# Three instead of four seven-product K-pairs in the query, key and pooled groups, and side splits in two steps

## The chip, the cores and the metric

The kernel runs on one core of a Trainium2 chip. The metric is the device time of one execution in microseconds; lower is better. The engines are named as in the profile: PE (TensorE matrix products, PEld its weight loads), DVE (VectorE), ACT (ScalarE), POOL (GpSimd) and SP (the queue that issues the DMAs). Each engine works through its own instructions strictly in the order in which the program gives them.

## The reference

One decoder layer on 256 tokens of width 2048, all in float32:

```
h   = rms_norm(x)
proj = h @ w_in                      # 2048 x 13312: q,k,v of attention A, u, q,k,v of C, 3 gates
ya  = softmax attention (8 heads of 128)
yb  = sliding-window means minus identity, one 256x256 map per group
yc  = stick-breaking attention (8 heads of 128)
m   = sum_b sigmoid(gate_b) * (y_b @ w_br_b)
x   = x + m @ w_out
h   = rms_norm(x)
x   = x + (silu(h @ w_gate) * (h @ w_up)) @ w_down       # 2048 x 5632
out = rms_norm(x)
```

## The kernel before

Each float32 operand is split into a high part that PE can take (fp32r) and the low rest, and a product is made of three PE instructions: high by high, low by high, high by low. Such an instruction has 128 rows, 128 columns of weights (here the activations) and 512 columns that stream (here the weight matrix).

The work is a list of groups; a group is one block of output columns over all of K. Most use the plain form (class `Group`). The groups of two 512-column blocks at once (class `Squares`: query A, key A and u of the first projection, the gates of branches b and c, and gate and up of the SwiGLU) run over eight pairs of K-tiles. A pair of kind `N` makes eight 128x512 products, thus 24 PE instructions, from one loaded raw tile: one high split on ACT (L446, 128x2048), one low split on DVE (L452, 128x2048). A pair of kind `W` makes seven products, thus 21 instructions, in two units: `Wp` (9) and `Ws` (12). It needs three sums of the raw weights on DVE (L442, L443, L444), two high splits (1536 and 2048 wide) and two low splits (1536 and 2048 wide), and of the activations four difference blocks where `N` needs two (`differences`, L150 to L170). The kinds of the eight pairs stand in two strings:

```
FFN_KINDS = "NNWNWNWN"
GATE_KINDS = "NWNWNWWN"
```

The first, with three `W`, holds for the SwiGLU groups, the second, with four, for every `Squares` group of w_in.

A `Squares` group collects its sums in seven of the eight PSUM banks; the eighth is left for side work. The first two blocks are freed early, by `squares_early` (ACT L474, DVE L475, L476).

What surrounds the groups is the list `side`: generators entered with `beside(gen, after, lag)`. After each unit on PE, `step_side` takes the first generator that is due and runs it to its next `yield`; its instructions land at that place in each engine's order. Side work is the activations' differences (`add_differences`, one K-pair a step), the attention heads, the pooling, the turning of `m` and of the hidden state (`turn` in `br`, L898, and in `output`, L954), and the end of each SwiGLU block (`finish`, L1001). The last three transpose on PE into a free bank and then split out of that bank: ACT writes the high part (L108), DVE subtracts it (L109), and the bank is free once both have read it. Between units the loop also issues the splits of units up to four ahead (`high` on ACT, `low` on DVE).

The order of the stages is: value A, then query A, key A and u (`Squares`), the projections of branch C (plain, with attention A and pooling beside them), gates and branch products, `output`, then eleven SwiGLU blocks in four parts, each with its share of the down projection.

Of the kernel before, what the change touches and what calls it, by code (L numbers as in the profile page):

```python
# [51 lines left out]
def trunk(ctx: ExitStack, tc: tile.TileContext, x, norm_mix, norm_ffn, w_in, w_pool, pool_scale,  # L52
# [43 lines left out]
    def f32(ap):  # L96
        return ap.bitcast(F32)
# [7 lines left out]
    def split(hi, lo, src, scale=None):  # L105
# [4 lines left out]
        else:  # L110
            nc.scalar.activation(hi, src, AF.Copy, scale=scale)
            nc.vector.scalar_tensor_tensor(lo, src, scale, f32(hi), OP.mult, OP.subtract)

    def branch():
        return slot([HEADS, SEQ], F32R), slot([HEADS, SEQ], F32R)

# [10 lines left out]
    class Halves:  # L127
# [22 lines left out]
        def differences(self, p, a):  # L150

            e = wk().rearrange("p (n s) -> p n s", s=P)
            n = 4 if self.kinds[p] == "W" else 2
            if n == 2:
                nc.vector.tensor_tensor(e[:, 0:2], a[:, :, 0], a[:, :, 1], OP.subtract)
            else:
                f = a.rearrange("p k t s -> p (k t) s")
                nc.vector.tensor_tensor(e[:, 0:2], f[:, 1:2].to_broadcast([P, 2, P]), f[:, 0:4:3], OP.subtract)
                nc.vector.tensor_tensor(e[:, 2], f[:, 0], e[:, 1], OP.subtract)
                nc.vector.tensor_tensor(e[:, 3], f[:, 2], e[:, 2], OP.subtract)  # L160
            for i, (tile, used) in enumerate(self.tiles):
                if used + 2 * n <= 16:
                    break
            else:
                i = len(self.tiles)
                tile, used = (late_slot if late and i < 1 else slot)([16, P], F32R), 0
                self.tiles.append(None)
            self.tiles[i] = tile, used + 2 * n
            self.ext[p] = tile, used, n
            split(tile[:, used:used + n], tile[:, used + n:used + 2 * n], e[:, 0:n])  # L170

        def add_differences(self, p):
            a = wk()
            hi, lo = self.pair(p)
            nc.vector.tensor_tensor(a.rearrange("p (k s) -> p k s", k=2), f32(hi), f32(lo), OP.add)
            self.differences(p, a.rearrange("p (k t s) -> p k t s", k=2, t=NT))

        def fill(self, p, pt, scales):

            a = wk()  # L180
            for j in range(2):
                k = slice(j * SEQ, (j + 1) * SEQ)
                nc.scalar.activation(a[:, k], pt[:, k], AF.Copy, scale=scales[j])
            split(*self.pair(p), a.rearrange("p (k s) -> p k s", k=2))
            self.differences(p, a.rearrange("p (k t s) -> p k t s", k=2, t=NT))


    xt = [slot([D_MODEL]) for _ in range(NT)]
# [65 lines left out]
    rstd1 = [st1[:, t, 9:10] for t in range(NT)]  # L254
    rstd2 = [st2[:, t, 9:10] for t in range(NT)]

    xT = Halves(GATE_KINDS)

    def prepare_x(kt):
        transposed(xT(kt), [xt[t][:, kt * P:(kt + 1) * P] for t in range(NT)], ncols[:, kt:kt + 1])  # L260
# [6 lines left out]
        side.append([clock[0] + after, lag, gen])  # L267

    def step_side():
        for e in side:  # L270
            if e[0] <= clock[0]:
                side.remove(e)
                try:
                    e[0] = clock[0] + (next(e[2]) or e[1])
                    side.append(e)
                except StopIteration:
                    pass
                return True
        return False

    def finish_side():
        while side:
# [298 lines left out]
    def proj_in(col, after, before=None, turned=False):  # L581
        return Group(lambda: xT, range(KT), w_in, 0, col, after, before, turned=turned)

    def in_pair(c0, finish, then=None):

        early = []

        def load(raw, p):
            nc.sync.dma_start(raw.rearrange("p j n c -> p j (n c)"),
                              w_in[2 * p * P:2 * (p + 1) * P, c0:c0 + 2 * CH].rearrange("(j p) c -> p j c", p=P))  # L590

        def begin(b):
            early.append(squares_early(b))

        def end(b):
            yield from finish(squares_end(b, early[0]))

        def before():
            cap[0] = 9

        def after(b):
            beside(end(b), after=2, lag=1)
            if then:
                then()

        return Squares(lambda: xT, load, after, begin, before, GATE_KINDS)


    live = {}
# [229 lines left out]
            yield  # L839

    def start_block():
        xT.tiles, xT.ext = [], {}
        make_bias()
        live["ya"] = branch()
        for hp in range(HEADS // 2):
            beside(block_attention(hp), after=8 + 4 * hp, lag=3)
        beside(pooling(), after=16, lag=2)
# [17 lines left out]
    def gate_pair(i, b):  # L865

        def finish(c):
            for t in range(NT):
                for n in range(2):
                    nc.scalar.activation(c[t][n], c[t][n], AF.Sigmoid, scale=rstd1[t])  # L870
            for n in range(2):
                gates[2 * i + n] = [c[t][n] for t in range(NT)]
            yield

        return in_pair(7 * WIDTH + b * D_MODEL + 2 * i * CH, finish)

    def br(n, b, plain=False):
        key = ("ya", "yb", "yc")[b]

        def lhs():  # L880
            y = live[key]
            return lambda kt: (y[0][:, kt, :], y[1][:, kt, :])

        def before():
            if n == 0 and b == 0:
                finish_side()
                open_late()
                beside((xT.add_differences(p) for p in range(KT // 2)), after=4, lag=2)
            if n % 2 == 0 and b == 0:
                both = slot([2, NT, CH])  # L890
                m.extend([both[:, i, t] for t in range(NT)] for i in range(2))

        def turn():
            for i in range(2):
                pt = bank()
                for j in range(4):
                    c = (2 * i + j // 2) * P
                    nc.tensor.transpose(pt[:, j * P:(j + 1) * P], m[n][j % 2][:, c:c + P], ident)  # L898
                split(*mT[0].pair(2 * n + i), pt.rearrange("p (k s) -> p k s", k=2))
                yield  # L900

        def after(acc):
            if b == 2 and n == 0:
                mT.append(Halves())
            for t in range(NT):
                g = gates[n][t]
                if plain:
                    nc.scalar.activation(g, g, AF.Sigmoid)
                if b == 0:
                    nc.vector.tensor_mul(m[n][t], acc[t], g)  # L910
                else:
                    nc.vector.tensor_mul(g, acc[t], g)
                    nc.vector.tensor_add(m[n][t], m[n][t], g)
            if b == 2:
                beside(turn(), after=4 if n < 2 else 2, lag=1)

        return Group(lhs, range(HEADS), w_br[b], 0, n * CH, after, before, span=4 if b else 2)
# [18 lines left out]
    def output(n):  # L936
        xr = []

        def before():
            if n == 0:  # L940
                h.extend(slot([D_MODEL]) for _ in range(NT))
                hT.append(Halves(FFN_KINDS))
                nc.scalar.preload_act_table(AF.Sqrt)
            for t in range(NT):
                xr.append(wk())
                nc.sync.dma_start(xr[t], x[toks(t), cols(n)])

        def turn():
            for i in range(2):
                pt = bank()  # L950
                kts = [4 * n + 2 * i + j for j in range(2)]
                for j, kt in enumerate(kts):
                    for t in range(NT):
                        nc.tensor.transpose(pt[:, j * SEQ + t * P:j * SEQ + (t + 1) * P], h[t][:, kt * P:(kt + 1) * P], ident)  # L954
                hT[0].fill(2 * n + i, pt, [ncols[:, 16 + kt:17 + kt] for kt in kts])
                yield

        def after(acc):
            for t in range(NT):
                nc.vector.tensor_add(h[t][:, cols(n)], acc[t], xr[t])  # L960
                square_sum(st2[:, t, n:n + 1], h[t][:, cols(n)])
            beside(turn(), lag=1)
            if n == 3:
                beside(norm_2(), after=4)

        return Group(lambda: mT[0], range(KT), w_out, 0, n * CH, after, before, span=4)
# [10 lines left out]
    def swiglu(f, last):  # L977
# [10 lines left out]
        def finish(b):  # L988
# [8 lines left out]
            for k in range(2):  # L997
                pt = bank()
                for i in range(2):
                    for t in range(NT):  # L1000
                        nc.tensor.transpose(pt[:, i * SEQ + t * P:i * SEQ + (t + 1) * P],  # L1001
                                            c[t][1][:, (2 * k + i) * P:(2 * k + i + 1) * P], ident)
                split(a[:, 2 * k:2 * k + 2, :], a[:, 4 + 2 * k:6 + 2 * k, :], pair(pt))
                if k == 0:
                    yield
            ready.add(f)
# [94 lines left out]
    startup[7] = lambda: next(norm_1, None)  # L1101
    stick_constants()
    beside((f() for f in (window_shares,)), after=10)
    beside((xT.add_differences(p) for p in range(KT // 2)), after=7, lag=2)
    run(in_order(groups), startup)


# [22 lines left out]
```

## Time and profile before

| | |
|---|---|
| median of 3 runs | 1563.03 us (1562.87 to 1563.2) |
| the profiled execution | 1563.04 us, its span 1561.2 us |
| PE busy, PEld busy | 1539.8 us (99%), 1291.0 us (83%) |
| DVE busy | 1161.6 us (74%) |
| ACT busy | 778.7 us (50%) |
| mean granted clock of PE | 0.996 of full speed |

The span runs from the first to the last instruction; about 1.8 us of the profiled time lie around it. A busy PE in this profile is not a PE at its peak, since the ends of matmuls are modelled: whether PE lost time is seen in how many instructions of one kind a stretch holds.

### The profile page before, as it was taken

What the parts mean: (1) busy time and instruction counts of PE and PEld (TensorE: products, weight loads), DVE (VectorE), ACT (ScalarE), POOL (GpSimd) and SP (SyncE); (2) the same over time, 40 slices, a digit from 0 to 9 for tenths busy, and PEclk for the clock granted to TensorE, in tenths of its full rate; (3) what the DMA queues carried; (4) which work ended last, traced back from release to release, by engine and by line L of the source; (5) the groups of instructions that cost most, each with busy time, mean ns of one, the idle gap of its engine ahead of it and who ended that gap; (6) DMA issues with size and microseconds to landing.
All of it is one profiled execution on the core that took longest, in us unless ns stands there. A gap on an engine that the chain in (4) does not pass through costs nothing.

```text
span 1561.2 us, 18182 instructions
## 1 busy us (share of the span) xinstructions
PE 1539.8 (99%) x7331; PEld 1291.0 (83%) x7331; DVE 1161.6 (74%) x1110; ACT 778.7 (50%) x741; POOL 39.3 (3%) x94
## 2 busy tenths in 40 slices
PE   9989999999999999999999999999999999999997
PEld 7868899988888888888888778888888888888886
DVE  6899856665478898978566898568885779857775
ACT  7545654346555545545454555344553345534452
POOL 0004000011100000000000000000000000000000
PEclk9989999999999999999999999999999999999999
DMA  9445744454545646738654556555575555755551
GB/s 358 155 166 187 244 161 167 159 188 149 172 162 194 238 139 238 251 126 293 206 178 159 175 203 233 171 188 183 196 243 179 176 190 183 256 175 189 189 215 54
DMA packets 138307, 300.05 MB, mean 192 GB/s; under 512 B 6464, under 2 KB 8048, under 8 KB 138096
## 3 DMA queue, kind: packets, MB, share of 16 engines
q1 hardware_dynamic: 137456, 297.44, 55.6%
q8 instruction: 57, 0.93, 0.2%
q0 software_dynamic: 304, 1.06, 0.2%
q10 hardware_dynamic: 464, 0.40, 0.1%
q14 instruction: 26, 0.21, 0.0%
HBM read 296.77 MB, written 2.11 MB: 191 GB/s over the span
## 4 chain that ended last, share of the span: by engine, by line
PE 89%; DVE 6%; issue 2%; ACT 2%; DMA 0%; ACTq 0%; DVEq 0%
PE bank L467 41%; PE bank L354 13%; PE bank L355 13%; PE bank L359 13%; DVE slot L452 2%; PE bank L382 2%; PE bank L374 2%; PE bank L376 2%; ACT slot L446 1%; DVE slot L442 1%; DVE slot L335 1%; PE bank L1001 1%; DVE slot L443 0%; PE bank L672 0%; DVE slot L109 0%
## 5 line engine op out<-in xcount | busy, mean ns | idle before, releaser
L467 PE MATMUL bank<-slot,slot 128*128 128x512 f32 x2913 | 690.8, 392 | 6.5 <-ACT slot L446 2.3
L467 PEld LDWEIGHTS bank<-slot,slot 128*128 128x128 f32 x2913 | 547.7, 189 | 123.5 <-DVE slot L452 3.0
L446 ACT ACTIVATE slot<-slot 128x2048 fp32r<-128x2048 f32 (+1 forms) x205 | 359.3, 1783 | 245.4 <-DVE slot L444 117.1
L452 DVE TENSOR_TENSOR slot<-slot,slot 128x2048 fp32r<-128x2048 f32 (+1 forms) x205 | 433.5, 2129 | 61.0 <-ACT slot L446 43.9
L354 PE MATMUL bank<-slot,slot 128*128 128x512 f32 (+1 forms) x936 | 365.1, 391 | 0.0
L355 PE MATMUL bank<-slot,slot 128*128 128x512 f32 (+1 forms) x936 | 362.4, 388 | 0.0
L335 DVE TENSOR_TENSOR slot<-slot,slot 128x1024 fp32r<-128x1024 f32 (+2 forms) x189 | 307.3, 1644 | 52.7 <-ACT slot L327 20.0
L327 ACT ACTIVATE slot<-slot 128x1024 fp32r<-128x1024 f32 (+2 forms) x189 | 256.5, 1391 | 55.1 <-PE bank L355 35.6
L359 PE MATMUL bank<-slot,slot 128*128 128x512 f32 (+1 forms) x936 | 236.6, 387 | 0.0
L354 PEld LDWEIGHTS bank<-slot,slot 128*128 128x128 f32 x936 | 175.8, 188 | 35.2 <-ACT slot L327 0.2
L355 PEld LDWEIGHTS bank<-slot,slot 128*128 128x128 f32 x936 | 175.9, 188 | 34.9
L359 PEld LDWEIGHTS bank<-slot,slot 128*128 128x128 f32 x936 | 174.9, 188 | 36.0
L467 PE MATMUL bank<-slot,late 128*128 128x512 f32 x360 | 101.0, 392 | 0.0
L108 ACT ACTIVATE slot<-bank 128x512 fp32r<-128x512 f32 x38 | 22.6, 595 | 135.5 <-PE bank L1001 78.3
L109 DVE TENSOR_TENSOR slot<-bank,slot 128x512 fp32r<-128x512 f32 x38 | 26.3, 691 | 79.1 <-ACT slot L108 79.0
L467 PEld LDWEIGHTS bank<-slot,late 128*128 128x128 f32 x360 | 67.0, 188 | 13.8
L442 DVE TENSOR_TENSOR slot<-slot 128x1024 f32<-128x1024 f32 x61 | 74.4, 1219 | 0.3 <-PE bank L359 0.2
L374 PE MATMUL bank<-slot,slot 128*128 128x256 f32 x256 | 64.0, 288 | 0.0
L376 PE MATMUL bank<-slot,slot 128*128 128x256 f32 x256 | 62.7, 283 | 0.0
L991 ACT ACTIVATE wk<-wk,st 128x512 f32<-128x512 f32 x22 | 14.7, 717 | 74.8 <-DVE wk L485 74.8
L1036 DVE TENSOR_TENSOR slot<-bank,slot 128x512 f32<-128x512 f32 x30 | 19.6, 686 | 42.6 <-PE bank L359 42.6
L376 PEld LDWEIGHTS bank<-slot,slot 128*128 128x128 f32 x256 | 49.1, 192 | 0.0
(168 smaller groups left out, 818.1 us busy)
## 6 DMA issues: line engine op xcount, KB each, us to landing
slot<-in_w_in_dram SPq DMA_DIRECT2D x103, 1024.0 KB, 5.1
slot<-in_w_gate_dram SPq DMA_DIRECT2D x88, 512.0 KB, 3.9
slot<-in_w_up_dram SPq DMA_DIRECT2D x88, 512.0 KB, 4.8
slot<-in_w_down_dram SPq DMA_DIRECT2D x44, 1024.0 KB, 5.2
slot<-in_w_out_dram SPq DMA_DIRECT2D x16, 1024.0 KB, 6.2
slot<-in_w_br_a_dram SPq DMA_DIRECT2D x8, 1024.0 KB, 5.2
slot<-in_w_br_b_dram SPq DMA_DIRECT2D x8, 1024.0 KB, 5.2
slot<-in_w_br_c_dram SPq DMA_DIRECT2D x8, 1024.0 KB, 5.2
```

The lines of the kernel that those rows point to most:

```text
L327: nc.scalar.activation(self.w[0][:, k], self.g.raw[self.i][:, k], AF.Copy)
L335: nc.vector.tensor_tensor(lo[:, k], raw[:, k], f32(hi[:, k]), OP.subtract)
L354: nc.tensor.matmul(acc[:, c], hi[:, toks(t)], whi[:, j, c], start=i + j == 0, stop=False)
L355: nc.tensor.matmul(acc[:, c], lo[:, toks(t)], whi[:, j, c], start=False, stop=False)
L359: nc.tensor.matmul(acc[:, c], hi[:, toks(t)], wlo[:, j, c], start=False, stop=i + j == n - 1)
L374: nc.tensor.matmul(o, whi[:, j, w], hi, start=i + j == 0 and c % 2 == 0, stop=False, skip_group_check=True)
L376: nc.tensor.matmul(o, whi[:, j, w], lo, start=False, stop=False, skip_group_check=True)
L382: nc.tensor.matmul(o, wlo[:, j, w], hi, start=False, stop=i + j == n - 1 and c % 2 == 1, skip_group_check=True)
L442: nc.vector.tensor_tensor(s[:, 0:2], raw[:, 0:1].to_broadcast([P, 2, CH]), raw[:, 1:3], OP.add)
L446: nc.scalar.activation(hi, src, AF.Copy)
L452: nc.vector.tensor_tensor(lo, src, f32(hi), OP.subtract)
L467: nc.tensor.matmul(g.banks[b], x, w[:, k, :], start=start, stop=g.left[b] == 0)
```

## The change

The groups of query A, key A and u take `FFN_KINDS`: one pair less in seven-product form in each, so nine PE instructions of 128x512 more in all. The gate groups keep `GATE_KINDS`, for which the differences are made anew in `start_block`, as they were before. Splits in side work are cut at a `yield`: the ACT part in one step, the DVE part in a later one. In `turn` of `br` (its first two column blocks) and in `finish` of a SwiGLU block that is not the last of its part, ACT copies the bank twice, once as the high part and once as float32 into a work tile, and DVE subtracts from the work tile. `step_side` may run two due generators after a unit, each once. The differences become one generator with two steps for each pair.

```diff
+    def split_later(hi, lo, src):
+
+        a = wk()
+        nc.scalar.activation(hi, src.rearrange("p (k s) -> p k s", k=2), AF.Copy)
+        nc.scalar.activation(a, src, AF.Copy)
+        yield
+        nc.vector.tensor_tensor(lo, a.rearrange("p (k s) -> p k s", k=2), f32(hi), OP.subtract)
...
-            split(tile[:, used:used + n], tile[:, used + n:used + 2 * n], e[:, 0:n])
+            hi = tile[:, used:used + n]
+            nc.scalar.activation(hi, e[:, 0:n], AF.Copy)
+            yield
+            nc.vector.tensor_tensor(tile[:, used + n:used + 2 * n], e[:, 0:n], f32(hi), OP.subtract)
...
+        def all_differences(self):
+            for p in range(KT // 2):
+                yield from self.add_differences(p)
+                yield
...
-            split(*self.pair(p), a.rearrange("p (k s) -> p k s", k=2))
-            self.differences(p, a.rearrange("p (k t s) -> p k t s", k=2, t=NT))
+            hi, lo = self.pair(p)
+            v = a.rearrange("p (k s) -> p k s", k=2)
+            nc.scalar.activation(hi, v, AF.Copy)
+            yield
+            nc.vector.tensor_tensor(lo, v, f32(hi), OP.subtract)
+            yield from self.differences(p, a.rearrange("p (k t s) -> p k t s", k=2, t=NT))
...
-    xT = Halves(GATE_KINDS)
+    xT = Halves(FFN_KINDS)
...
     def step_side():
-        for e in side:
-            if e[0] <= clock[0]:
+        for e in [e for e in side if e[0] <= clock[0]][:2]:
+            if e in side:
                 side.remove(e)
                 try:
                     e[0] = clock[0] + (next(e[2]) or e[1])
                     side.append(e)
                 except StopIteration:
                     pass
-                return True
-        return False
...
-    def in_pair(c0, finish, then=None):
+    def in_pair(c0, finish, then=None, kinds=FFN_KINDS):
...
-        return Squares(lambda: xT, load, after, begin, before, GATE_KINDS)
+        return Squares(lambda: xT, load, after, begin, before, kinds)
...
-        xT.tiles, xT.ext = [], {}
+        xT.kinds, xT.tiles, xT.ext = GATE_KINDS, [], {}
...
-        return in_pair(7 * WIDTH + b * D_MODEL + 2 * i * CH, finish)
+        return in_pair(7 * WIDTH + b * D_MODEL + 2 * i * CH, finish, kinds=GATE_KINDS)
...
-                split(*mT[0].pair(2 * n + i), pt.rearrange("p (k s) -> p k s", k=2))
+                if n < 2:
+                    yield from split_later(*mT[0].pair(2 * n + i), pt)
+                else:
+                    split(*mT[0].pair(2 * n + i), pt.rearrange("p (k s) -> p k s", k=2))
                 yield
...
-                hT[0].fill(2 * n + i, pt, [ncols[:, 16 + kt:17 + kt] for kt in kts])
+                yield from hT[0].fill(2 * n + i, pt, [ncols[:, 16 + kt:17 + kt] for kt in kts])
                 yield
...
-                split(a[:, 2 * k:2 * k + 2, :], a[:, 4 + 2 * k:6 + 2 * k, :], pair(pt))
+                parts = a[:, 2 * k:2 * k + 2, :], a[:, 4 + 2 * k:6 + 2 * k, :]
+                if last:
+                    split(*parts, pair(pt))
+                else:
+                    yield from split_later(*parts, pt)
...
-    beside((xT.add_differences(p) for p in range(KT // 2)), after=7, lag=2)
+    beside(xT.all_differences(), after=7, lag=1)
```

Line numbers of the changed kernel are higher: the low split is L470 there (L452 before), the sums L460 to L462 (L442 to L444), the Square matmul L485 (L467), the split of a difference L181 (L109), the turning transposes L916 (L898), the SwiGLU's L1022 (L1001).

The first place is DVE at the start of the query group. In these rows L175 rebuilds a pair of activations, L155 or L158 to L160 make its differences, L109 splits them, and L452 with a 2048 or 1536 wide tile is the low split of a unit's weights. Before:

```order
L442 TENSOR_TENSOR slot_550<-slot_442 128x1024
L443 TENSOR_TENSOR slot_550<-slot_550,slot_442 128x512
L444 TENSOR_TENSOR slot_550<-slot_550,slot_442 128x512
L452 TENSOR_TENSOR slot_556<-slot_391,slot_524 128x2048
L452 TENSOR_TENSOR slot_572<-slot_442,slot_554 128x1536
L175 TENSOR_TENSOR wk_588<-slot_236 128x512
L155 TENSOR_TENSOR wk_590<-wk_588 128x256
L109 TENSOR_TENSOR slot_547<-wk_590,slot_547 128x256
L452 TENSOR_TENSOR slot_594<-slot_550,slot_570 128x2048
```

After:

```order
L470 TENSOR_TENSOR slot_549<-slot_390,slot_524 128x2048
L181 TENSOR_TENSOR slot_545<-wk_543,slot_545 128x256
L460 TENSOR_TENSOR slot_566<-slot_509 128x1024
L461 TENSOR_TENSOR slot_566<-slot_566,slot_509 128x512
L462 TENSOR_TENSOR slot_566<-slot_566,slot_509 128x512
L470 TENSOR_TENSOR slot_572<-slot_439,slot_547 128x2048
L186 TENSOR_TENSOR wk_586<-slot_236 128x512
L166 TENSOR_TENSOR wk_588<-wk_586 128x256
L167 TENSOR_TENSOR wk_588<-wk_586,wk_588 128x128
L168 TENSOR_TENSOR wk_588<-wk_586,wk_588 128x128
L470 TENSOR_TENSOR slot_593<-slot_509,slot_570 128x1536
L181 TENSOR_TENSOR slot_545<-wk_588,slot_545 128x512
```

The split of the differences no longer follows the differences at once: a low split of weights stands between L168 and L181, where before L109 followed L155 directly. The first sums belong to the third pair instead of the second.

The second place is PE in the second gate pair of branch c, beside which `turn` transposes the first two blocks of `m`. Before, from the second set of transposes to the third, around the `Ws` unit of the second K-pair:

```order
L898 MATMUL bank_5411<-ident,slot_3631 128x128 x4
L467 MATMUL bank_5367<-slot_5317,late_3703 128x512 x2
L467 MATMUL bank_5430<-slot_5317,late_3703 128x512 x2
L467 MATMUL bank_5433<-slot_5317,late_3703 128x512 x2
L467 MATMUL bank_5362<-slot_5317,slot_125 128x512 x2
L467 MATMUL bank_5367<-slot_5319,late_3703 128x512
L467 MATMUL bank_5430<-slot_5319,late_3703 128x512
L467 MATMUL bank_5433<-slot_5319,late_3703 128x512
L467 MATMUL bank_5362<-slot_5319,slot_125 128x512
L898 MATMUL bank_5442<-ident,slot_3631 128x128 x4
```

After, the end of the same unit:

```order
L485 MATMUL bank_5350<-slot_5302,late_3686 128x512
L485 MATMUL bank_5408<-slot_5302,late_3686 128x512
L485 MATMUL bank_5411<-slot_5302,late_3686 128x512
L485 MATMUL bank_5345<-slot_5302,slot_125 128x512
L916 MATMUL bank_5420<-ident,slot_3614 128x128 x4
L916 MATMUL bank_5429<-ident,slot_3614 128x128 x4
L485 MATMUL bank_5340<-slot_5334,slot_177 128x512 x4
```

Two generators are due after this unit, so two sets of transposes, each into a bank of its own, stand back to back; before they stood one to a unit.

The third place is ACT at that same point; L446 (now L464) are the high splits of weights, L108 (now L117 and L118) read the transposed bank. Before:

```order
L108 ACTIVATE slot_5390<-bank_5411 128x2x256
L446 ACTIVATE slot_5418<-slot_5393 128x2048
L446 ACTIVATE slot_5422<-slot_5321 128x2048
L108 ACTIVATE slot_5447<-bank_5442 128x2x256
L446 ACTIVATE slot_5480<-slot_5355 128x1536
```

After:

```order
L464 ACTIVATE slot_5396<-slot_5377 128x2048
L464 ACTIVATE slot_5400<-slot_5304 128x2048
L117 ACTIVATE slot_5425<-bank_5420 128x2x256
L118 ACTIVATE wk_5426<-bank_5420 128x512
L117 ACTIVATE slot_5373<-bank_5429 128x2x256
L118 ACTIVATE wk_5434<-bank_5429 128x512
L464 ACTIVATE slot_5469<-slot_5338 128x1536
```

The two high splits of the `Ws` unit and of the pair behind it stand ahead of the first bank's two copies, and the second bank's copies follow at once.

## Rows read from the trace of the kernel before

**Rows 1.** The page: busy time by engine, and the granted clock in 40 slices.

```profile
PE 1539.8 (99%) x7331; PEld 1291.0 (83%) x7331; DVE 1161.6 (74%) x1110; ACT 778.7 (50%) x741; POOL 39.3 (3%) x94
...
PEclk9989999999999999999999999999999999999999
```

**Rows 2.** Busy time by stretch: window, length, then engines' busy us (instructions), clock, DMA.

```profile
494.98:535.78 40.80, 40.80 (x181) 33.78 (x181) 36.47 (x26) 21.73 (x14) 0.00 (x0) 1.00 0.68 245
...
53.82:98.90 45.08, 41.51 (x168) 32.87 (x167) 39.72 (x38) 22.99 (x18) 0.00 (x0) 0.92 0.43 146
74.72:113.30 38.58, 32.59 (x119) 24.91 (x118) 34.48 (x32) 16.70 (x12) 0.00 (x0) 0.87 0.48 165
88.20:93.20 5.00, 5.00 (x13) 3.98 (x12) 4.93 (x5) 1.37 (x2) 0.00 (x0) 0.50 0.49 153
864.00:905.00 41.00, 37.53 (x165) 29.71 (x164) 38.35 (x31) 23.30 (x17) 0.00 (x0) 1.00 0.60 204
...
200.00:300.00 100.00, 100.00 (x817) 99.15 (x816) 61.27 (x99) 44.91 (x76) 1.83 (x3) 1.00 0.43 146
```

**Rows 3.** Whom PE waited for, whole run: us in total, times, longest.

```profile
PE bank L467 <- ACT slot L446: 2.3, 1, 2.3
PE bank L467 <- ACT wk L474: 1.8, 1, 1.8
...
PE bank L1001 <- DVE wk L994: 1.5, 2, 1.2
PE bank L467 <- DVE slot L452: 1.4, 3, 0.7
```

**Rows 4.** Timeline of DVE in the query group: start, us, line, shapes, [idle before, releaser].

```profile
57.69 0.69 DVE L175 TENSOR_TENSOR wk<-slot 128x512 f32<-128x512 f32 x1
...
59.32 0.42 DVE L109 TENSOR_TENSOR slot<-wk,slot 128x256 fp32r<-128x256 f32 x1 [0.48 <-ACT slot L108]
59.67 2.29 DVE L452 TENSOR_TENSOR slot<-slot,slot 128x2048 fp32r<-128x2048 f32 x1
...
67.66 1.22 DVE L442 TENSOR_TENSOR slot<-slot 128x1024 f32<-128x1024 f32 x1
...
70.25 1.75 DVE L452 TENSOR_TENSOR slot<-slot,slot 128x1536 fp32r<-128x1536 f32 x1
...
74.59 0.69 DVE L175 TENSOR_TENSOR wk<-slot 128x512 f32<-128x512 f32 x1
...
77.08 0.69 DVE L109 TENSOR_TENSOR slot<-wk,slot 128x512 fp32r<-128x512 f32 x1 [0.70 <-ACT slot L108]
77.69 2.29 DVE L452 TENSOR_TENSOR slot<-slot,slot 128x2048 fp32r<-128x2048 f32 x1
```

**Rows 5.** Whom DVE waited for between 53.82 and 98.90 us.

```profile
DVE slot L452 <- ACT slot L446: 2.5, 4, 1.4
DVE slot L109 <- ACT slot L108: 2.4, 4, 0.8
```

**Rows 6.** Timeline around the third transposes of `turn` in a gate pair.

```profile
692.52 3.72 ACT L446 ACTIVATE slot<-slot 128x2048 fp32r<-128x2048 f32 x2 [0.82 <-DVE slot L444]
...
694.07 0.68 DVE L109 TENSOR_TENSOR slot<-bank,slot 128x512 fp32r<-128x512 f32 x1
...
694.81 0.66 PE L898 MATMUL bank<-ident,slot 128*128 128x128 f32 x4 [0.98 <-DVE slot L109]
...
696.14 0.58 ACT L108 ACTIVATE slot<-bank 128x512 fp32r<-128x512 f32 x1
```

**Rows 7.** Timeline of the first SwiGLU block and of its end.

```profile
860.55 0.21 ACT L233 ACTIVATE st<-st 128x2 f32<-128x2 f32 x1 [3.64 <-DVE st L232]
...
864.02 4.49 DVE L452 TENSOR_TENSOR slot<-slot,slot 128x2048 fp32r<-128x2048 f32 x2 [2.27 <-ACT slot L446]
...
897.85 0.33 PE L1001 MATMUL bank<-ident,wk 128*128 128x128 f32 x1 [1.15 <-DVE wk L994]
...
903.37 0.66 PE L1001 MATMUL bank<-ident,wk 128*128 128x128 f32 x4 [1.54 <-DVE slot L109]
```

More of the change, by code (lines that the diff above doesn't have):

```diff
@@ L183, in fill @@
                 nc.scalar.activation(a[:, k], pt[:, k], AF.Copy, scale=scales[j])
-            split(*self.pair(p), a.rearrange("p (k s) -> p k s", k=2))
-            self.differences(p, a.rearrange("p (k t s) -> p k t s", k=2, t=NT))
+            hi, lo = self.pair(p)
[3 more added lines that the diff above has]
+            nc.vector.tensor_tensor(lo, v, f32(hi), OP.subtract)
+            yield from self.differences(p, a.rearrange("p (k t s) -> p k t s", k=2, t=NT))
     xt = [slot([D_MODEL]) for _ in range(NT)]
@@ L887, in before @@
                 open_late()
-                beside((xT.add_differences(p) for p in range(KT // 2)), after=4, lag=2)
+                beside(xT.all_differences(), after=4, lag=1)
             if n % 2 == 0 and b == 0:
```

## The prediction

> **What bounds the kernel now.** I read the page first: PE is busy 99% of the span, DVE 74%, ACT 50%, and the granted clock is full but for one slice [rows 1]. A busy PE says little here, so the second view is the count of PE instructions by stretch. A gate group that nothing disturbs, from 494.98 us on, takes 40.80 us for its 180 products of 128x512, 0.2267 us each; in it DVE is busy for 36.47 of the 40.80 us, and PE still loses nothing [rows 2]. That is the measure: a group with four seven-product pairs fits under PE when it is alone on DVE, with about 4 us to spare. With 0.2267 us for each product, I look for stretches that hold too few of them. Three have a loss that this change touches.
>
> The large one is the query group and the start of the key group. From 74.72 to 113.30 us PE starts 119 products, worth 27.0 us, in 38.58 us: 11.6 us are lost [rows 2]. Part of it is the clock: it is granted at 0.87 on average there, and from 88.20 to 93.20 at 0.50, the lower of its two levels (1.2 GHz), where 13 products take 5.00 us; the level fell after PE had waited [rows 2]. The waits themselves are for ACT's high split (2.3 us), for ACT's early copy (1.8) and for DVE's low splits (1.4) [rows 3], and behind all of them is DVE. From the first low split of the query group (53.82) to the last one (98.90) it needs 45.08 us where PE's 180 products need 40.8. In these 45.08 us it is busy for 39.72 and waits for ACT for 4.9 [rows 2, 5]. It is fuller than in the undisturbed group because the activations' differences run beside it, and it waits because each difference is split at once: DVE makes it, ACT copies it, DVE waits 0.48 or 0.70 us and subtracts [rows 4].
>
> The second is the first SwiGLU block and its end, 864 to 905 us. Of 165 PE instructions 157 are products (35.6 us) and eight are transposes (about 0.8 us in all; four show 0.66 with their modelled end), together 36.4 of 41.00 us: 4.6 us are lost [rows 2, 7]. The third is small: in a gate pair, transposes wait 0.98 us for a bank that DVE reads last [rows 6].
>
> **The change part by part.** *Nine products more.* One pair less in each of three groups, three instructions for each: 9 x 0.2267 = +2.0 us on PE, which is full. Nothing hides them.
>
> *Less DVE work in the query group.* A pair that goes from `W` to `N` drops the three sums (67.66 to 70.25, 2.59 us) and one 1536 wide low split (1.75); the 2048 wide one stays [rows 4]. That is 4.34 us. One pair of activations in this stretch needs two differences in place of four: with its split it takes 1.98 us (57.69 to 59.67) in place of 3.10 (74.59 to 77.69), and without the waits inside 1.50 in place of 2.40, so 0.9 less [rows 4]. DVE's work falls from 39.72 to 34.5 us, while PE's own time for the group grows to 183 x 0.2267 = 41.5. That is 83% against the 89% of the undisturbed group (36.47 of 40.80), which lost nothing [rows 2].
>
> *Two-step splits.* In the new order a weight split stands between a difference and its own split, so ACT's copy (0.4 to 0.6 us) lies under a low split of 1.75 or 2.29 us, and the 2.4 us of waits for L108 go [rows 4, 5]. The 2.5 us for L446 can stay: ACT is in order too, and its high split of a unit still stands behind the copy of a difference that DVE makes late. Then 34.5 + 2.5 = 37.0 us of DVE against 41.5 of PE: DVE gains 4.5 us on PE over the group where it lost 4.3. What is late next is that high split. If I follow the new order by these durations, from the same start, the high split of the second `W` pair is ready just when PE wants it, and the low splits of the second and third `W` pair come up to 0.5 us late. The va groups ahead also lose waits of this kind, so DVE starts earlier, by perhaps 2 us. I take 0.5 us for what is left of the 11.6. Bounds: 0, and 5 if both waits for ACT stay (2.3 + 1.8 [rows 3]) and cost some clock. Key and u had no loss worth naming, and lose DVE work too.
>
> *The turned `m`.* Two sets of transposes now stand back to back after a `Ws` unit, when seven banks hold the group's sums. The second set needs the bank of the first, and that bank is free after two copies on ACT (0.58 each), which stand behind two 2048 wide high splits. At the same place before, these two took 3.72 us from 692.52 on, after a wait for DVE's sums, and the copy began at 696.14 [rows 6]. PE would be there at about 694.2. If the high splits run as late as before, the bank is free at 697.3, 3.1 us later; if ACT is ready, after the two copies and their signals, about 1.3. The sums no longer stand behind DVE's read of a bank, so ACT comes earlier: I take 2.1. The old wait of 0.98 goes. Net +1.1 (+0.3 to +2.1). Queued behind PE's wait are only products whose operands are ready, and nobody waits for those so soon.
>
> *The first SwiGLU block.* The second transposes waited 1.54 us for a bank that DVE released at its turn [rows 7]. Now ACT alone frees it, and the set stands three units, not one, behind the first. That wait goes. The first transposes' wait of 1.15 us for L994 [rows 7] I keep: that DVE instruction still stands behind a low split that waits for an in-order high split. The rest (4.6 less 1.54 and about 1.5) are waits for DVE's splits and early sums; DVE has fewer waits in the turning of the hidden state now, and by its new order it comes to the norm about 2 us earlier, where ACT had idled 3.64 us and DVE then 2.27 [rows 7]. Of this 1.5 I count 1.2. Gain 2.7 (0 to 4.6).
>
> The Trainium skill speaks against the copies: VectorE: DVE Perf Modes, Rules for kernel authors, lets an elementwise operation on a matmul's output read PSUM directly, and copies to SBUF first only where many operations follow; here one follows. No row here has DVE's subtract from such a copy; the nearest, on a work tile, takes 0.69 us against 0.68 from a bank [rows 4, 6], which agrees that nothing is saved on DVE itself. By that rule the copies would bring only ACT work, and the gain of 2.7 would shrink to 1.2.
>
> The 18 extra copies (4 in `turn`, 2 in each of 7 SwiGLU blocks) are 10.4 us of ACT; what hides them is ACT's idle time, 17.7 of the 41.00 us from 864 on [rows 2]. Without that cover they would cost PE the bank, as at the turned `m`.
>
> *Two generators after one unit.* Attention and pooling come closer together between 200 and 300 us; the pooling's small weight DMAs stand earlier on SP, ahead of one load of w_in that used to precede them. PE is full there, DVE at 61 and ACT at 45 of 100 us [rows 2]. The units ahead are split well before PE needs them. I take +0.3 (0 to 2). No gain is possible where nothing is lost.
>
> **The sum**, against the profiled 1563.04 us (span 1561.2 and 1.8 around it; the median of the runs is 1563.03, the same): -11.6 + 0.5 + 2.0 + 1.1 - 2.7 + 0.3 = -10.4, so **1552.6 us**. All bounds at their best give -11.6 + 2.0 + 0.3 - 4.6 = -13.9 (1549.1), all at their worst -11.6 + 5 + 2.0 + 2.1 + 2 = -0.5 (1562.5).
>
> **The rivals.** *ACT takes DVE's place as the holder of banks and splits*: query gains, the SwiGLU block gains nothing, the turn costs 2.1 more than nothing: -11.6 + 0.5 + 2.0 + 2.1 + 0.3 = -6.7, 1556.3. For it: both new holds are ACT's, in order. Against: ACT is idle for 17.7 of the 41.00 us from 864 on [rows 2]. Chance 0.14. (The rule on reading PSUM directly, in VectorE: DVE Perf Modes of the Trainium skill, points to this case.) *The stall moves on*: DVE keeps up through the query group, but ACT's order or the key group's first sums bring 5 us back: 1557.1. For it: the longest single wait was ACT's [rows 3]; against: behind that wait stood DVE. Chance 0.12. *The change doesn't do what it says*: the query stall isn't DVE's load, all of it stays, and only the other terms count: +0.7, 1563.7. Against it stands the undisturbed gate group, with four `W` pairs and no loss [rows 2]. Chance 0.06. *Slower*: the paired side steps. PE is in order, so a side matmul whose softmax or pooled operand is not ready holds all products behind it. One such wait costs 1.15 to 1.5 us, as L1001's did [rows 7]; from 12 of them on (13.5 us: the gain of 10.4 and 3.1 more) the kernel is slower, at eighteen of 1.15 us about 1573. For it: the stretch from 200 to 300 us has some thirty such steps; against: PE there has not one gap, and DVE 39% idle time [rows 2]. Chance 0.05. *Better than forecast*, all terms near their best: 1549, chance 0.05.
>
> **How the numbers follow.** The forecast (1550 to 1555.5) has 0.58. The range 1548.5 to 1558.5 takes in the first two rivals and the better case and leaves out the third and the slower one. A change under 0.2% (3.1 us) can't be told from none with this kernel. Faster by more: 0.58 + 0.14 + 0.12 + 0.05 = 0.89; same 0.06; slower 0.05.
>
> **What would show it.** Right: between 74 and 113 us about 0.2267 us for each product and no clock at 0.50; DVE's waits for L108's successor near zero; a wait of about 2 us at the doubled transposes; no wait of the SwiGLU's second transposes. Wrong: a low clock still in the query group; PE waiting for ACT's high splits there; gaps between 200 and 300 us.

## The result and the profile after

The changed kernel takes 1552.95 us (median of 4 runs, 1551.3 to 1553.25) against 1563.07 us (4 runs, 1562.87 to 1563.2): a ratio of 0.9933 with a 95% interval of 0.9916 to 0.995, faster by 10.1 us. The profiled execution is the quickest of the four, 1551.3 us with a span of 1549.6; the span of the profiled execution before was 1561.2. The page of the changed kernel, where [rows 1] stand for before:

```profile
PE 1535.2 (99%) x7340; PEld 1291.1 (83%) x7340; DVE 1144.7 (74%) x1096; ACT 781.5 (50%) x756; POOL 41.1 (3%) x94
...
PEclk9999999999999999999999999999999999999999
```

PE's share is 99% as before; its busy time is 4.6 us less although it has nine instructions more, and the slice with a clock under full is gone. Where the time came from must again be read by stretches. Windows of the changed kernel (window, length, then engines' busy us and instructions, clock, DMA), of the stretches in [rows 2] and of two others:

```profile
47.16:90.40 43.24, 43.24 (x193) 35.81 (x192) 37.84 (x38) 23.12 (x19) 0.00 (x0) 1.00 0.54 194
53.82:98.90 45.08, 45.08 (x200) 37.36 (x199) 39.64 (x40) 24.34 (x19) 0.00 (x0) 1.00 0.52 188
74.72:113.30 38.58, 38.58 (x176) 31.96 (x175) 34.46 (x30) 21.51 (x18) 0.00 (x0) 1.00 0.54 192
195.00:310.00 115.00, 115.00 (x881) 111.49 (x880) 74.05 (x123) 50.26 (x86) 5.14 (x6) 1.00 0.49 162
```

From 74.72 to 113.30 us PE now starts 176 instructions where it started 119, at a full clock. Of the 176, 168 are products (38.1 us at 0.2267), eight are transposes: nothing is lost. To set stretches beside each other I use one measure from here on: the *lost time* of a stretch is what the distances from one start on PE to the next have above the usual one (0.2267 us between products). These values are good to some 0.1 us. From one profiled execution to the next the first 40 us alone differ by up to 0.9 us of lost time (3.7 to 4.6 in the nine traces), so two spans are compared no better than that.

| stretch, us | lost before | lost after |
|---|---|---|
| 74 to 120, query and key | 11.9 | 0.3 |
| 195 to 310, attention A and pooling | 1.5 | 1.4 |
| 680 to 720, `turn` of `m` | 1.6 | 2.3 |
| 840 to 910, first SwiGLU block | 5.0 | 2.8 |

With the nine products (+2.0) the four rows make -11.2 of the -11.6 by which the span fell. The waits of PE, whole run, where [rows 3] stand for before:

```profile
PE bank L916 <- ACT wk L118: 1.9, 1, 1.9
PE bank L1022 <- DVE wk L1015: 1.5, 2, 1.1
...
PE bank L485 <- DVE wk L493: 0.4, 1, 0.4
```

PE's waits for ACT's high split and DVE's low splits are gone; the longest is now the one at the doubled transposes.

**Query group.** The timeline of DVE (start, us, line, shapes, [idle before, releaser]), against [rows 4]:

```profile
47.16 2.28 DVE L470 TENSOR_TENSOR slot<-slot,slot 128x2048 fp32r<-128x2048 f32 x1
49.36 0.42 DVE L181 TENSOR_TENSOR slot<-wk,slot 128x256 fp32r<-128x256 f32 x1
...
56.19 1.75 DVE L470 TENSOR_TENSOR slot<-slot,slot 128x1536 fp32r<-128x1536 f32 x1
57.86 0.68 DVE L181 TENSOR_TENSOR slot<-wk,slot 128x512 fp32r<-128x512 f32 x1
...
61.90 4.49 DVE L470 TENSOR_TENSOR slot<-slot,slot 128x2048 fp32r<-128x2048 f32 x2 [2.29 <-ACT slot L464]
...
75.26 2.29 DVE L470 TENSOR_TENSOR slot<-slot,slot 128x2048 fp32r<-128x2048 f32 x1 [2.56 <-ACT slot L464]
```

Every difference's split (L181) follows a weight split with no wait. The waits for the high split (L464) are 4.9 us in two pieces; in [rows 5] they were 2.5. And the first low split of the group stands at 47.16, not 53.82 us, while PE enters the group at the same time: at 55.20 us before,

```profile
55.20 24.36 PE L467 MATMUL bank<-slot,slot 128*128 128x512 f32 x106
```

and at 55.18 us now. PE's row shows one unbroken run, and 240 products in the 54.40 us from 55.18 to 109.58 are 0.2267 us each:

```profile
55.18 54.57 PE L485 MATMUL bank<-slot,slot 128*128 128x512 f32 x240
109.58 0.60 PE L658 MATMUL bank<-ident,wk 128*128 128x128 f32 x4
```

**Turn.** The two back-to-back sets of transposes, where [rows 6] stood:

```profile
679.49 5.09 ACT L464 ACTIVATE slot<-slot 128x1536 fp32r<-128x1536 f32 x3
...
683.13 0.60 PE L916 MATMUL bank<-ident,slot 128*128 128x128 f32 x4
...
684.47 0.60 ACT L117 ACTIVATE slot<-bank 128x512 fp32r<-128x512 f32 x1
684.94 0.61 ACT L118 ACTIVATE wk<-bank 128x512 f32<-128x512 f32 x1
685.60 0.42 PEld L916 LDWEIGHTS bank<-ident,slot 128*128 128x128 f32 x4 [2.11 <-ACT wk L118]
685.60 0.66 PE L916 MATMUL bank<-ident,slot 128*128 128x128 f32 x4 [1.87 <-ACT wk L118]
```

ACT's high splits run to 684.58, the first copy starts only at their end (684.47), and the second set waits 1.87 us for the second copy.

**SwiGLU.** The end of the first block, where [rows 7] stood:

```profile
885.13 2.29 DVE L470 TENSOR_TENSOR slot<-slot,slot 128x2048 fp32r<-128x2048 f32 x1 [2.01 <-ACT slot L464]
...
887.34 1.41 DVE L1015 SCALAR_TENSOR_TENSOR wk<-wk,st,wk 128x512 f32<-128x512 f32 x2
...
888.14 0.33 PE L1022 MATMUL bank<-ident,wk 128*128 128x128 f32 x1 [1.14 <-DVE wk L1015]
...
888.80 0.55 PE L1022 MATMUL bank<-ident,wk 128*128 128x128 f32 x3 [0.33 <-DVE wk L1015]
...
895.53 0.69 DVE L120 TENSOR_TENSOR slot<-wk,slot 128x512 fp32r<-128x512 f32 x1
...
897.38 0.60 PE L1022 MATMUL bank<-ident,wk 128*128 128x128 f32 x4
```

The first transposes wait as before, the second ones (897.38) not at all. L120 is DVE's subtract from the work tile.

### The profile page after: what moved, and what is told of

Read it like the earlier page. It is cut to its first block, busy times and chain, and to the rows that moved or that the text cites. A ratio compares the mean times of both kernels' runs of the same rounds, so it can differ in the third digit from the quotient of the medians.

```text
span 1549.6 us, 18224 instructions
## 1 busy us (share of the span) xinstructions
PE 1535.2 (99%) x7340; PEld 1291.1 (83%) x7340; DVE 1144.7 (74%) x1096; ACT 781.5 (50%) x756; POOL 41.1 (3%) x94
## 4 chain that ended last, share of the span: by engine, by line
PE 94%; DVE 2%; ACT 1%; issue 1%; DMA 0%; ACTq 0%; DVEq 0%
PE bank L485 44%; PE bank L372 14%; PE bank L373 14%; PE bank L377 14%; PE bank L400 2%; PE bank L392 2%; PE bank L394 2%; DVE slot L470 1%; ACT slot L464 1%; PE bank L1022 1%; PE bank L690 0%; DMA slot<-in_x_dram 0%; PE bank L658 0%; DVE slot L460 0%; PE bank L691 0%
## 5 line engine op out<-in xcount | busy, mean ns | idle before, releaser
L485 PE MATMUL bank<-slot,slot 128*128 128x512 f32 x2922 | 686.6, 390 | 0.4 <-DVE wk L493 0.4
L485 PEld LDWEIGHTS bank<-slot,slot 128*128 128x128 f32 x2922 | 547.0, 188 | 113.6 <-DVE wk L493 0.8
L470 DVE TENSOR_TENSOR slot<-slot,slot 128x2048 fp32r<-128x2048 f32 (+1 forms) x202 | 427.9, 2134 | 89.0 <-ACT slot L464 70.4
L464 ACT ACTIVATE slot<-slot 128x2048 fp32r<-128x2048 f32 (+1 forms) x202 | 353.7, 1789 | 196.5 <-DVE slot L462 71.8
L485 PE MATMUL bank<-slot,late 128*128 128x512 f32 x360 | 100.6, 391 | 0.0
L485 PEld LDWEIGHTS bank<-slot,late 128*128 128x128 f32 x360 | 67.1, 188 | 13.7
L460 DVE TENSOR_TENSOR slot<-slot 128x1024 f32<-128x1024 f32 x58 | 70.7, 1219 | 2.9 <-PE bank L377 2.8
L109 DVE TENSOR_TENSOR slot<-bank,slot 128x512 fp32r<-128x512 f32 x20 | 13.8, 691 | 61.9 <-ACT slot L108 61.8
L117 ACT ACTIVATE slot<-bank 128x512 fp32r<-128x512 f32 x18 | 10.8, 599 | 82.6 <-PE bank L1022 69.1
```

Of the source, the lines that this page charges most:

```text
L460: nc.vector.tensor_tensor(s[:, 0:2], raw[:, 0:1].to_broadcast([P, 2, CH]), raw[:, 1:3], OP.add)
L464: nc.scalar.activation(hi, src, AF.Copy)
L470: nc.vector.tensor_tensor(lo, src, f32(hi), OP.subtract)
L485: nc.tensor.matmul(g.banks[b], x, w[:, k, :], start=start, stop=g.left[b] == 0)
```

## The experiments

Each ran five rounds beside the kernel before, whose median was 1563.03 us beside the first four and 1563.1 beside the last three. The theory is the prediction's: DVE's load makes the query stall (called load), and the other terms stand as priced there. The rivals are named with each.

**1. The kinds alone.** The kernel before with three seven-product pairs in query, key and u; splits, `turn` and SwiGLU as before.

```diff
-    xT = Halves(GATE_KINDS)
+    xT = Halves(FFN_KINDS)
...
-    def in_pair(c0, finish, then=None):
+    def in_pair(c0, finish, then=None, kinds=FFN_KINDS):
...
-        return Squares(lambda: xT, load, after, begin, before, GATE_KINDS)
+        return Squares(lambda: xT, load, after, begin, before, kinds)
...
-        xT.tiles, xT.ext = [], {}
+        xT.kinds, xT.tiles, xT.ext = GATE_KINDS, [], {}
```

(The gate groups pass `GATE_KINDS`.)

> Only the kinds change (three seven-product pairs in query, key and u); the splits and the side order stay as before. Theory 1, the query group's stall is DVE's load: its DVE needs about 34.5 us of work and 4.9 us of waits, 39.4, against 41.5 us of PE, so the stall goes but for about 1 us, and the two other losses stay: 1563.1 - 11.6 + 1 + 2.0 = 1554.5 us, with 0 to 3 us lost between 74 and 113 us. Theory 2, the stall is made by DVE's and ACT's waits for each other in the one-step splits: half of the stall or more stays, 1559 us or above.

Measured: 1556.01 us (1555.6 to 1556.2), ratio 0.9954 (0.9941 to 0.9966). The clock stays full, but 2.9 us are lost from 74 to 120 us. The waits of PE, and the window of the stall:

```profile
PE bank L467 <- DVE wk L475: 1.6, 2, 1.3
PE bank L1001 <- DVE slot L109: 1.5, 1, 1.5
...
PE bank L467 <- DVE slot L452: 0.6, 2, 0.4
```

```profile
74.72:113.30 38.58, 36.83 (x162) 29.30 (x161) 32.35 (x29) 22.99 (x19) 0.00 (x0) 1.00 0.52 175
```

PE still waits, mainly at two places: 0.4 us for a low split late in the query group, and 1.3 us (L475, DVE's early sum) at the start of the key group. The lost time falls by 9.0 us, the nine products cost 2.0: 7.0 us, what was measured. The loss lies in the expected 0 to 3 us; the time is 1.5 us above the expected 1554.5.

**2. All but the kinds.** The changed kernel with four seven-product pairs again.

```diff
-    xT = Halves(FFN_KINDS)
+    xT = Halves(GATE_KINDS)
...
-    def in_pair(c0, finish, then=None, kinds=FFN_KINDS):
+    def in_pair(c0, finish, then=None, kinds=GATE_KINDS):
```

> The changed kernel with four seven-product pairs again in query, key and u, so the two-step splits and the two generators alone. Theory 1 (load): DVE needs 39.7 us of work and about 2.5 us of waits, 42.2, against PE's 40.8, so 2 to 5 us of the query stall stay, nine products (2.0 us) go: 1552.95 - 2.0 + 4 = 1555 us (1553 to 1557). Theory 2 (waits alone made the stall): no stall is left, 1551.0 us.

Measured: 1556.77 us (1556.53 to 1558.19), ratio 0.9962 (0.9949 to 0.9974). From 74 to 120 us 7.1 us are lost. PE's waits there (L470 late in the query group, L492 at the start of the key group), and a window behind the one for L492:

```profile
PE bank L485 <- ACT wk L492: 1.9, 1, 1.9
PE bank L485 <- DVE slot L470: 1.9, 1, 1.9
```

```profile
102.00:105.40 3.40, 3.40 (x10) 2.63 (x9) 3.37 (x4) 1.27 (x1) 0.00 (x0) 0.50 0.00 0
```

Here DVE's full load is back, and so are waits and 3.4 us at the lower clock. So the loss of 11.9 us becomes 2.9 with the kinds alone, 7.1 with the steps alone, 0.3 with both. Part of two of these is the clock: products that start 0.427 us apart at a granted 0.50 make up about 4.4 of the 11.9 and 1.6 of the 7.1 us, and none of the 2.9. Without that it is 7.5, 2.9, 5.5 and 0.3. Neither edit does it alone, and the kinds do more; what each changes on DVE stands below, in the part on the prediction.

**3. The two turns apart.** In the changed kernel the first two `turn` generators start at different units, so that no two sets of transposes meet.

```diff
-                beside(turn(), after=4 if n < 2 else 2, lag=1)
+                beside(turn(), after=(4, 5, 2, 2)[n], lag=1)
```

> The changed kernel with the turning of the second block of m one unit later, so that no two sets of transposes share a unit. Theory: PE's wait for the second set's bank (1.9 us for ACT, 2.04 us lost in the changed kernel's trace) goes and nothing replaces it, 1552.95 - 2.0 = 1551 us. Rival: the wait was only where ACT's lateness showed, and a wait of 1 us or more comes back at the next set, 1552 to 1553 us.

Measured: 1549.71 us (1549.35 to 1550.12), ratio 0.9913 (0.99 to 0.9927). PE's wait at L916 is gone, and from 680 to 720 us 0.3 us are lost in place of 2.3. That is 2.0 us; the median fell by 3.2. The profiled executions of the two kernels are 1.5 us apart, for the start of this one lost 0.5 us more. For the other 1.2 us of the median experiments 4 and 5 give a likely cause.

**4. SwiGLU banks read by DVE again.** In the changed kernel `finish` splits out of the bank, as before. This takes out two things at once: the copies, and the `yield` in `split_later`, so that the second transposes come closer behind the first.

```diff
-                if last:
-                    split(*parts, pair(pt))
-                else:
-                    yield from split_later(*parts, pt)
+                split(*parts, pair(pt))
```

> The changed kernel with the one-step split out of the bank (ACT, then DVE, no second copy) in every SwiGLU block. Theory: the second transposes of the first block's end wait again for DVE's read, about 1.5 us, 1554.5 us, and nothing else changes. Rival, that the second copy and its delay bring nothing because DVE is no longer late: 1552.95 us, no wait for DVE's split there.

Measured: 1555.05 us (1553.27 to 1556.08), ratio 0.9946 (0.9933 to 0.9958), 2.1 more than the changed kernel. The wait of the second transposes is back (PE's waits, and the timeline there):

```profile
PE bank L1022 <- DVE slot L109: 1.5, 1, 1.5
```

```profile
890.52 0.33 PE L1022 MATMUL bank<-ident,wk 128*128 128x128 f32 x1 [1.15 <-DVE wk L1015]
...
895.30 0.68 DVE L109 TENSOR_TENSOR slot<-bank,slot 128x512 fp32r<-128x512 f32 x1
...
896.04 0.66 PE L1022 MATMUL bank<-ident,wk 128*128 128x128 f32 x4 [1.54 <-DVE slot L109]
```

From 840 to 910 us 4.6 us are lost, 1.8 more than in the changed kernel. Which of the two things does it, this run can't tell. The second set starts 5.5 us behind the first here, 1.5 of them in the wait, and 9.2 us behind it in the changed kernel (888.14 to 897.38), where DVE's subtract was over at 896.22: a bank that DVE had read would have been free 1.2 us before the second set, too. So by this trace the later place is enough, and what the copies add here is not shown. (In experiment 6 the order is tighter: there the second set starts at 895.34, before DVE's subtract at 895.61, and ACT's copies, over at 893.94, are what freed the bank.)

The trace of experiment 4 shows something else, at the doubled transposes, which are the same as in the changed kernel. Windows before and after PE's wait there ends:

```profile
684.00:687.00 3.00, 1.13 (x8) 0.89 (x7) 3.00 (x3) 2.35 (x3) 0.00 (x0) 0.92 1.00 366
687.00:690.00 3.00, 3.00 (x10) 2.41 (x9) 3.00 (x4) 2.48 (x3) 0.00 (x0) 0.52 0.27 109
```

PE comes out of the wait at about half the clock, as in experiment 2. From 680 to 720 us 3.8 us are lost, 1.6 more than in the profiled execution of the changed kernel, whose clock stayed full there.

**5. The float32 copy first.** In the changed kernel ACT copies the bank once, into the work tile, and makes the high part from that copy, so the bank is free one copy earlier.

```diff
-        nc.scalar.activation(hi, src.rearrange("p (k s) -> p k s", k=2), AF.Copy)
         nc.scalar.activation(a, src, AF.Copy)
+        nc.scalar.activation(hi, a.rearrange("p (k s) -> p k s", k=2), AF.Copy)
```

> The changed kernel, but the second copy is made first, from the bank, and the high part then from that copy in SBUF, so that a bank is held for one ACT read instead of two. Theory, that the doubled transposes wait for ACT's in-order reads of one bank: the wait of 2.04 us shrinks by one copy (0.58) to about 1.5 us; if the clock level falls after the longer wait only, another 1.3 us come back, so 1552.4 us without and 1551.1 us with that. Rival, that the wait is for ACT's high splits ahead of the copies and not for the copies: no change, 1552.95 us.

Measured: 1551.28 us (1550.95 to 1551.56), ratio 0.9923 (0.991 to 0.9935). Timeline at the second set:

```profile
684.54 0.57 ACT L117 ACTIVATE wk<-bank 128x512 f32<-128x512 f32 x1
...
685.17 0.66 PE L916 MATMUL bank<-ident,slot 128*128 128x128 f32 x4 [1.56 <-ACT wk L117]
```

The wait is only 0.31 us shorter, not the 0.58 of one copy: most of it is for the high splits ahead of the copies, as the rival had it. But the median falls by 1.7, and all five runs lie within 0.4 us of the profiled execution of the changed kernel. The other three executions of the changed kernel took 1.6 to 2.0 us longer. That fits a clock that fell behind this wait, as the trace of experiment 4 shows it, which cost 1.6 us there. In a trace of the changed kernel itself it wasn't seen, and the mean clock doesn't settle it: it is 0.997 to 0.998 in these three and 0.999 in the profiled one, but 0.998 in three runs of experiment 5 as well. A slower start, worth up to 0.9 us in these traces, could be part of it.

**6. A later end of the SwiGLU block.** Experiment 3, and in `finish` two units, not one, between DVE's last product of the block and its transposes.

```diff
                 nc.vector.scalar_tensor_tensor(c[t][1], c[t][1], rstd2[t], c[t][0], OP.mult, OP.mult)
-            yield
+            yield None if last else 2
```

> The kernel with the turns of m apart (1549.7 us), and in each SwiGLU block that is not the last of its part the first transposes one unit later (12 products, 2.7 us). Theory, that these transposes only come too early for DVE's late product (1.86 us lost at the end of the first block, nothing at the others): 1549.7 - 1.9 = 1547.8 us. Rival, that DVE is behind there and the next product waits instead: 1549 to 1549.7 us.

Measured: 1547.51 us (4 runs, 1547.33 to 1547.6), ratio 0.9899 (0.9884 to 0.9914). The waits of PE behind the start of the program come down to one:

```profile
PE bank L485 <- DVE wk L493: 0.4, 1, 0.4
```

The loss from 840 to 912 us falls to 0.9 us. This is the best version, 1.0% under the kernel before and 5.4 us under the changed one.

**7. Four seven-product pairs in the SwiGLU too.** Experiment 3 with `GATE_KINDS` in all eleven blocks: 33 products less (7.5 us), and 4.34 us of DVE more in each block ([rows 4], as in the prediction).

```diff
-                hT.append(Halves(FFN_KINDS))
+                hT.append(Halves(GATE_KINDS))
...
-        return Squares(lambda: hT[0], load, after, begin, before)
+        return Squares(lambda: hT[0], load, after, begin, before, GATE_KINDS)
```

> The kernel with the turns of m apart (1549.7 us), with four seven-product pairs instead of three in the eleven SwiGLU blocks too: 33 products less (-7.5 us), and 4.34 us more of DVE work in each. Theory 1 (DVE's load decides): a SwiGLU block's DVE is busy 35.0 to 35.7 us in 41.5 now, it would be 39.3 to 40.0 of 40.8 and about 2 us of waits for ACT more, over PE's time, so 1 us or more is lost in each block but is partly made good in the down groups between: 1548 to 1556 us, with losses in the blocks of 6 us or more in all. Rival (the two-step splits alone had made room): nothing is lost, 1542.2 us.

Measured: 1563.89 us (11 runs, 1562.05 to 1567.8), ratio 1.0008 (0.9999 to 1.0018), 14.2 us more than experiment 3. PE's waits, whole run:

```profile
PE bank L1022 <- DVE wk L1015: 7.9, 8, 1.7
PE bank L485 <- DVE wk L502: 3.1, 4, 0.8
PE bank L485 <- DVE slot L470: 2.2, 2, 2.0
PE bank L485 <- ACT slot L464: 2.1, 1, 2.1
PE bank L485 <- ACT wk L492: 1.9, 1, 1.9
```

From 840 to 912 us 12.7 us are lost, and 13.7 more from there to 1540 (1.8 in experiment 3). The direction is that of load, but the size is well outside the 1548 to 1556 expected of it. The largest item, 7.9 us, is not for splits of weights but at the transposes that end a block, which experiment 6 moves one unit back; four pairs together with that edit were not tried, so 14.2 us is not the price of the load alone.

Not tried: the changed kernel with one generator per unit, since the differences of a gate pair then come behind the products that read them; and the SwiGLU's second transposes at their new place with DVE reading the bank.

## Why the prediction was right

The forecast was 1552.6 us, the median is 1552.95. By its own terms:

**Query stall, -11.6 and 0.5 left: right in size, its working wrong in four places that cancel.** The loss fell by 11.6 us. But the step "DVE's work falls from 39.72 to 34.5 us", with 2.5 us of waits to 37.0 against PE's 41.5, doesn't hold. DVE takes 43.24 us from the first low split of the group to the last, 37.84 of them busy and 4.9 in waits for L464: longer than PE's 41.5, not shorter. First, the 39.72 was too low. Before, the first of the four pairs had its sums ahead of 53.82, at 51.23 us (a later set of such sums is in [rows 4]), so three sets lay inside the window, and three lie inside it now. Windows from DVE's first work of the group (sums or low split) to its last low split, for the kernel before, the kinds alone and the steps alone:

```profile
51.23:98.90 47.67, 44.10 (x180) 35.02 (x179) 42.24 (x41) 23.73 (x19) 0.00 (x0) 0.93 0.46 156
```

```profile
49.59:93.35 43.76, 43.35 (x190) 35.00 (x189) 37.96 (x37) 22.39 (x18) 0.00 (x0) 1.00 0.53 188
```

```profile
47.67:94.18 46.51, 44.64 (x197) 36.44 (x196) 42.40 (x43) 25.03 (x20) 0.00 (x0) 1.00 0.48 162
```

| | DVE starts the group | takes | busy | lost, 74 to 120 |
|---|---|---|---|---|
| before | 51.23 | 47.67 | 42.24 | 11.9 |
| kinds alone | 49.59 | 43.76 | 37.96 | 2.9 |
| steps alone | 47.67 | 46.51 | 42.40 | 7.1 |
| both | 47.16 | 43.24 | 37.84 | 0.3 |

So the fall of 4.34 us that the prediction worked out is there (42.24 to 37.84). Second, the further 0.9 for the activations is not: before and after, this stretch rebuilds two pairs with four differences and two with two. Third, DVE's idle time did not fall to 2.5 us, it is 5.4 in both kernels: the waits for L108 went, those for ACT's high split doubled. Fourth, and on the other side, the term that I wrote down as "perhaps 2 us" is 4.1: DVE begins the group at 47.16 in place of 51.23 us, 8.0 us ahead of PE, and uses up that lead over the group. (Of the 6.7 us between the first low splits, 47.16 against 53.82, 2.6 are the sums that stood ahead of it.) That these four cancel is luck. That it takes less work and an early start together is what the table shows: the kinds take 4.3 to 4.6 us of work off, the steps bring the start 2.4 to 3.6 us forward. With the steps alone DVE starts only 0.5 us later than in the changed kernel, and 7.1 us are lost; with the kinds alone it has the changed kernel's work, and 2.9 are lost. The start was not changed by itself.

**Two-step splits.** DVE's waits for the differences' copies went to nothing, as forecast, and its waits for the high split doubled: what was late next was named rightly, its size not. The steps matter on their own: 2.6 us of lost time between experiment 1 and the changed kernel.

**Nine products, +2.0**: as counted; experiment 1's own sum closes with it.

**Turn, +1.1.** The new wait measured 1.87 us against 2.1, and the loss rose by 0.7 in the profiled execution. Missed was what follows: taking the wait out (experiment 3) gave 3.2 us of median, not 2.0. So this edit costs about 1.2 us more at the median than its wait; by experiments 4 and 5 that is most likely the clock, which no trace of the changed kernel shows.

**First SwiGLU block, -2.7.** It gained 2.2. The wait of the second transposes went, and experiment 4 brings it back at 1.8 us of lost time (2.1 in the median); the first wait stayed (1.14 us). Of the rest I had counted 1.2, and about 0.5 came. The prediction gave two reasons for the wait to go, that ACT alone frees the bank and that the set stands three units behind the first; by the trace the second is enough, and the first is not shown (experiment 4). So the copies may well bring only ACT work here: DVE's subtract takes 0.68 us from the work tile and 0.69 from a bank. The Trainium skill (VectorE: DVE Perf Modes, Rules for kernel authors) copies to SBUF first only where many operations follow. The changed kernel's trace doesn't contradict that; only in the order of experiment 6 do the copies free the bank ahead of DVE.

**Two generators after one unit, +0.3.** The losses from 195 to 310 us are 1.5 before and 1.4 after: nothing. Their price apart from the rest stays open.

The -10.4 of the sum stands beside -11.6 in the span and -10.1 in the median; the clock behind the doubled transposes would fit what lies between these two. That the median comes within 0.4 us of the forecast is thus partly luck. The signs that were named came: full clock and 0.2267 us for each product in the query group, no wait of DVE for the differences' copies, 1.87 us at the doubled transposes, none at the SwiGLU's second ones. Of the rivals, ACT did become the holder of a bank at the turn, but the SwiGLU gain stayed; no other stretch took up the stall, and no side step was seen to hold PE between 195 and 310 us.

## What to carry to other kernels

Where one engine feeds another through a long group, compare not only the work of both over the group but where the feeder stands when the group begins: with a lead of 8.0 us a DVE that was slower than PE over the whole group held nothing up here, and with almost the same lead (7.8 us) but 4.6 us more work it did. When an engine with a long in-order queue frees the last free bank, let the next user of that bank come later, or free it by an idler engine; which of the two paid here was not separated. Two users of that bank should not be due at one unit (3.2 us here). Four seven-product pairs cost nothing in an undisturbed gate group [rows 2], but 14.2 us when every SwiGLU block has them.

## What the runs showed of the hardware beyond that

A single wait of PE in an otherwise full stream can be paid for again. Behind waits with 2.0 us of lost time (experiments 2 and 4) the granted clock stood at 0.50, the lower level (1.2 GHz), for 3.4 us, in which about half the products start: 1.6 us more. It is not certain to happen: the profiled execution of the changed kernel had 2.0 us lost at the same place as experiment 4 and kept its clock, and so did the first wait of this size in experiment 2, at 87 us. Behind the wait with 1.7 us lost in experiment 5 the clock stayed full in the one trace there is.
